# First three attention units' scores between the last three query projections, first keys by halves, values queued later

## The chip, the cores and the metric

The kernel runs on one core of one Trainium2 chip. The metric is the device time of one execution in microseconds (us). Below, TensorE is the matrix engine (PE in the profile, PEld its weight loads), VectorE is DVE, ScalarE is ACT, GpSimd is POOL, and SyncE (SP) issues most DMAs. GpSimd issues DMAs too, from a software queue of its own. PSUM is the accumulator memory of eight banks into which TensorE writes.

## What is computed

One layer of a diffusion backbone over 1024 latent tokens and 256 context tokens of width 1024: a modulated norm, one input projection whose columns feed two head groups (retention in both directions, and differential attention), an output projection, and a gated MLP with a short convolution. The change concerns differential attention and what stands just before it:

```
def diff_attention(q, k, v, lam):
    # q (B,H,2,Lq,d), k (B,H,2,Lk,d), v (B,H,Lk,dv), scale = d ** -0.5
    def attend(qb):
        s = jnp.einsum('bhmqd,bhmkd->bhmqk', qb, k).astype(jnp.float32) * scale
        p = jax.nn.softmax(s, axis=-1)
        a = p[:, :, 0] - lam * p[:, :, 1]
        return jnp.einsum('bhqk,bhke->bhqe', a.astype(v.dtype), v)
```

There are 4 heads (H), each with two maps of width d = 64, values of width 128, 1024 queries and 1280 keys (256 of the context, 1024 latent). The queries are projections of the normalised tokens, turned by a rotary embedding.

## The kernel before

The program is one long stream. A scheduler puts the instructions of a stretch in an order of its own unless they are tied to each other (`order_only`, `in_order`), and adds every wait that the data or a reused buffer needs.

**The stretch ahead of attention.** `transposed` computes the queries of differential attention. For one head h and one half hf of the tokens (512 columns) it sums eight k steps into one PSUM tile `pl`; a k step is three matmuls (`passes`, L131 to L133), since every operand is split into a high and a low part (`hT` tokens, `whi` and `wlo` weights). This document writes (h, hf) for such a projection. The last three, `by_head[-TAIL:]` with TAIL = 3, are (2,1), (3,0) and (3,1). `rotated` then turns each of them: ScalarE copies two halves of 64 partitions of `pl` into `xb` (L429), VectorE forms `xa` from `pl` (L431), `xb` is multiplied (L432, on GpSimd for the last three), VectorE adds (L433), and `split_store` splits `xa` into `xhl` (ScalarE cast L416, subtraction L417) and stores it to `dq_d` in DRAM by a DMA of SyncE (L418).

While the projections run, a generator beside them (`beside`, one step per `tick`, one tick per k step) issues the work of the other head group. In the last stretch its pairs of retention chunks end with `turn`: TensorE transposes into `pyt` (L286), ScalarE casts into `yr` (L290), VectorE subtracts (L291), SyncE stores `yr` (L293). `yr` has one buffer, so a cast waits until the store of the pair before has read it.

**Attention.** It runs in 32 units, one for each head and each 128 queries; unit u has head u // 8 and query tile u % 8. The steps of a unit are named by letters in `OPS`: S1 and S0 are the scores of map 1 and map 0 on TensorE (L874, six matmuls into `pA`, 1280 columns in three banks, twice for the high and low part of the query), M1 and M0 VectorE's minimum over a row (L877, a reduction; the scores are negated), E1 and E0 ScalarE's exponential with the sum of a row (L881, output `p`), R the ratio (L885, L886), C the combination of both maps (L889), T1, T2, T0 transposes of the result in groups of 512, 256 and 512 columns (L894 into `pt`), K1, K2, K0 their copies by ScalarE (L900 into `aT`), V0 to V2 the products with the values (L906 into `pv`); the rest normalises, with a power on GpSimd (`ssa`, L921), and writes the unit's rows into `yT`. Each map has one `pA` of three PSUM banks (`pss`), so S1 of a unit waits for E1 of the unit before.

In the loop the order is written out: `TAU` gives each step a time in units of one period, `order` sorts the steps of a period, and `in_order(start)` ties the instructions of TensorE, VectorE, ScalarE and SyncE to it. GpSimd is not tied.

**Before the loop** the first two units' steps up to C are issued by a generator beside the last three projections: `early` lets 15 ticks pass, and at the next one issues S1, M1, S0, M0, E1, E0, R, C of unit 0 and of unit 1 at once. Where they then stand is the scheduler's choice.

**Loads.** `load(i)` reads from DRAM, by GpSimd's queue, what unit i needs anew: every fourth unit the queries of four units (`qhl`, L953), every eighth the keys (`ks`, L956) and the values (`va`, L959) of a head. For unit 0 the queries and keys come in two parts for each map (four DMAs of 256 KB and four of 320 KB), then the values (640 KB). They are issued behind `last_y[0]`, the last product of the retention group on GpSimd.

**Output weights.** `out_weights` loads the first half of the output projection by GpSimd's queue (`woraw`, L998, four buffers), and splits it (ScalarE cast L1004, GpSimd subtraction L1005). Its steps are taken one for each period from the twelfth on, behind step f; the DMAs hang on nothing but their buffers.

## Time and profile before

| what | us |
|---|---|
| median of 3 runs | 1386.81 |
| lowest and highest | 1386.27, 1386.91 |
| the profiled execution, its own time | 1387.61 |
| its span, first to last instruction | 1385.8 |
| TensorE busy | 1367.0 |
| VectorE busy | 998.0 |
| ScalarE busy | 734.5 |
| GpSimd busy | 302.5 |
| granted TensorE clock, mean | 0.999 |

The prediction shows lines of these views. A page line of busy times gives for each engine the busy time, its share of the span and the number of instructions. A line of waits gives the engine, its tile and line, behind the arrow what it waited for, and then the total, the number and the longest of such waits. A timeline line gives the start, the duration, the engine, the line, the operation, output and inputs, their sizes, how many were merged (x6), and in brackets the idle time before it and what ended that. A DMA line gives output and input, the queue (SPq, POOLq), the count, the size of one and the time from issue to landing. A line of windows gives the stretch, its length, the busy time of TensorE, of its weight loads, of VectorE, ScalarE and GpSimd with instruction counts, the granted clock, the DMA engines' busy share and the GB/s moved. All times of lines are counted from the span's start.

Attention begins near 454 us, its loop near 470 us, and it ends near 655 us.

### The profile page before, as it was taken

The numbers are of one execution on the slowest core, as the hardware profiler recorded it, in microseconds if no ns is written. First come the engines' busy times: TensorE is split into PE (matmuls) and PEld (weight loads), VectorE is DVE, ScalarE is ACT, GpSimd is POOL, SyncE is SP. The second block draws the span as 40 slices with busy tenths as digits, with TensorE's granted clock in tenths as the row PEclk, the third lists the DMA queues.
The fourth block names the chain that finished last, engine by engine and source line by source line (L and its number), as shares of the span: only waits on it lengthen the run. The fifth ranks groups of instructions, "written<-read, shape, count | busy, mean of one in ns | idle before, by whom it ended". The sixth has DMA issues, their size and how long they took to land. (4 is left out here: it accounts for less than half of the span.)

```text
span 1385.8 us, 19518 instructions
## 1 busy us (share of the span) xinstructions
PE 1367.0 (99%) x7066; PEld 1149.5 (83%) x7066; DVE 998.0 (72%) x1474; ACT 734.5 (53%) x1400; POOL 302.5 (22%) x323
## 2 busy tenths in 40 slices
PE   9999999999999999999999999999999999999997
PEld 6788888888988799998888788888888888888886
DVE  4655774424776898895458998887778777799857
ACT  4652322434665789987136654555445555454534
POOL 1310000002656423411200643222332220000001
PEclk9999999999999999999999999999999999999999
DMA  9546885454564778622410232332323325963523
GB/s 371 204 167 208 294 271 184 145 176 141 156 189 143 214 176 185 142 50 93 174 69 23 99 109 105 114 114 92 114 99 114 104 71 177 376 229 110 180 91 122
DMA packets 95625, 214.63 MB, mean 155 GB/s; under 512 B 9317, under 2 KB 29797, under 8 KB 95017
## 3 DMA queue, kind: packets, MB, share of 16 engines
q1 hardware_dynamic: 86792, 187.03, 39.4%
q0 software_dynamic: 8160, 24.91, 7.8%
q10 hardware_dynamic: 576, 1.44, 0.3%
q8 instruction: 56, 0.92, 0.3%
q14 instruction: 41, 0.33, 0.1%
HBM read 158.03 MB, written 55.31 MB: 154 GB/s over the span
## 5 line engine op out<-in xcount | busy, mean ns | idle before, releaser
L131 PE MATMUL pl<-hT,whi 128*128 128x512 f32 x256 | 105.8, 413 | 0.0
L131 PE MATMUL chain<-T,whi 128*128 128x512 f32 x264 | 103.0, 391 | 1.2 <-ACT ub L1305 0.9
L132 PE MATMUL chain<-T,whi 128*128 128x512 f32 x264 | 102.8, 389 | 0.0
L133 PE MATMUL chain<-T,wlo 128*128 128x512 f32 x264 | 102.4, 389 | 0.0
L133 PE MATMUL pl<-hT,wlo 128*128 128x512 f32 x256 | 100.3, 392 | 0.0
L132 PE MATMUL pl<-hT,whi 128*128 128x512 f32 x256 | 99.9, 390 | 0.0
L877 DVE TENSOR_REDUCE mt<-pA 128x1 f32<-128x1280 f32 x64 | 95.2, 1490 | 4.1 <-PE pA L874 2.4
L874 PE MATMUL pA<-ks,qhl 128*128 128x512 f32 (+1 forms) x384 | 89.7, 369 | 1.2 <-DVE xa L431 0.9
L131 PE MATMUL c<-whi,ghl 128*128 128x512 f32 x232 | 90.2, 389 | 0.0
L132 PE MATMUL c<-wlo,ghl 128*128 128x512 f32 x232 | 90.2, 389 | 0.0
L133 PE MATMUL c<-whi,ghl 128*128 128x512 f32 x232 | 90.2, 389 | 0.0
L881 ACT ACTIVATE p<-pA,mt 128x1280 f32<-128x1280 f32 x64 | 85.5, 1336 | 5.9 <-DVE mt L877 4.7
L1051 ACT CAST whi<-cmb 128x512 fp32r<-128x512 f32 x62 | 38.5, 622 | 80.5 <-PE chain L132 62.9
L874 PEld LDWEIGHTS pA<-ks,qhl 128*128 128x128 f32 x384 | 67.8, 189 | 13.8 <-DVE xa L431 1.3
L906 PE MATMUL pv<-va,aT 128*128 128x128 f32 x640 | 77.0, 275 | 0.1
L1211 POOL TENSOR_TENSOR cmb<-wrb 128x512 f32<-128x512 f32 x19 | 28.0, 1476 | 221.8 <-DMA wrb<-w_up 143.4
L1054 DVE TENSOR_TENSOR wlo<-cmb,whi 128x512 fp32r<-128x512 f32 x62 | 60.1, 970 | 20.3 <-ACT whi L1051 20.2
L906 PEld LDWEIGHTS pv<-va,aT 128*128 128x128 f32 x640 | 74.0, 192 | 0.7 <-DVE yT L935 0.3
L1051 ACT CAST whi<-wra 128x512 fp32r<-128x512 f32 x54 | 33.2, 623 | 71.8 <-PE third L132 42.3
L131 PE MATMUL third<-yT,whi 128*128 128x512 f32 x168 | 65.4, 389 | 0.0
L132 PE MATMUL third<-yT,whi 128*128 128x512 f32 x168 | 65.4, 389 | 0.0
L133 PE MATMUL third<-yT,wlo 128*128 128x512 f32 x168 | 65.4, 389 | 0.0
(328 smaller groups left out, 3855.2 us busy)
## 6 DMA issues: line engine op xcount, KB each, us to landing
wm<-w_mod SPq DMA_DIRECT2D x32, 512.0 KB, 5.1
raw<-w_in SPq DMA_DIRECT2D x27, 512.0 KB, 4.9
wra<-w_up SPq DMA_DIRECT2D x24, 512.0 KB, 3.2
wrb<-w_up SPq DMA_DIRECT2D x22, 512.0 KB, 3.5
W<-w_down SPq DMA_DIRECT2D x44, 256.0 KB, 6.1
ad<-s SPq DMA_DIRECT2D x20, 512.0 KB, 3.4
wra<-ad SPq DMA_DIRECT2D x20, 512.0 KB, 3.3
kvs<-kvg SPq DMA_DIRECT2D x36, 256.0 KB, 3.1
```

Source lines behind the costliest of these rows:

```text
L131: mm(ps, lh, rh, start=first, stop=False, skip_group_check=more)
L132: mm(ps, lh, rl, start=False, stop=False, skip_group_check=more)
L133: return mm(ps, ll, rh, start=False, stop=last, skip_group_check=more)
L874: mm(self.pa[m][:, c0:c1], self.q[:, m, i, qs], self.k[:, m, c0:c1], start=(i == 0), stop=(i == 1))
L877: nc.vector.tensor_reduce(out=self.mt[:, m : m + 1], in_=self.pa[m][:, :LK], axis=AX.X, op=ALU.min)
L881: nc.scalar.activation(self.p[m], self.pa[m][:, :LK], AF.Exp, scale=-1.0, bias=self.mt[:, m : m + 1], accum_out=self.s[:, m : m + 1])
L906: mm(self.pv, self.aT[:, c, :], self.v[:, c, :], start=(c == 0), stop=(c == NKT - 1))
L1051: cast = nc.scalar.copy(hi, src)
L1054: nc.vector.tensor_tensor(out=lo, in0=src, in1=r32(hi), op=ALU.subtract)
L1211: nc.gpsimd.tensor_tensor(out=s1, in0=b1, in1=b2, op=ALU.add)
```

## The change

- `early` now makes three units and issues their first steps at set ticks (`AHEAD`): the key is the tick, the text the steps, with the unit's number ahead of the letter. Only TensorE's order of the stretch is tied (`in_order(begin, (PE,))`). Two more ties are added: C of unit 1 behind the last rotation (`newest_read`), and R behind M0 of unit 0.
- In the loop some steps of units 0, 2 and 3 move (`MOVED`): S0 of unit 2 takes the place of its S1, which went ahead, K1 and T2 of unit 0 go behind E1 of unit 2, and T0 and K0 of unit 0 behind S1 of unit 3.
- The two last turned pairs take their `yr` from the free buffers of `sc` and `qq`, two tiles that the retention group no longer needs.
- For unit 0 the queries come as the columns of units 0 and 1 for one map, then that map's keys, then the same for the other map, and the columns of units 2 and 3 last; these DMAs are tied to this order.
- `load_values(0)` issues the values of head 0 behind the first product that GpSimd does for a rotation, where they stood behind the keys.
- The pools `wo`, `at` and `psa` wait for the single tile whose place they take (`reuse_waits="tile"`), where they waited for all of the pool before.
- Each load of output weights is issued behind the power of unit n - 6.

```diff
...
 EARLY = ("S1", "M1", "S0", "M0", "E1", "E0", "R", "C")
+AHEAD = {13: "S1 M1", 15: "S0 M0 E1 E0", 17: "1S1 1M1 R C", 19: "1S0 1M0 1E1 1E0 1R 1C", 22: "2S1"}
...
+MOVED = {("S1", 2): [("S0", 2)], ("S0", 2): [], ("K1", 0): [], ("T2", 0): [], ("E1", 2): [("E1", 2), ("K1", 0), ("T2", 0)], ("T0", 0): [], ("K0", 0): [], ("S1", 3): [("S1", 3), ("T0", 0), ("K0", 0)]}
 FORCE = (mybir.EngineType.PE, mybir.EngineType.DVE, mybir.EngineType.Activation, mybir.EngineType.SP)
...
 
-    def in_order(start):
+    def in_order(start, engines=FORCE):
         last = {}
         for ins in nc.cur_bb.bb.instructions[start:]:
-            if ins.engine not in FORCE:
+            if ins.engine not in engines:
                 continue
...
                         order_only(ins.ins, behind.ins)
-                yr = rt.tile([P, 2, 2, P], F32R, name="yr", bufs=1)
+                left = H * NT // 2 - 1 - (self.h * NT // 2 + self.g)
+                yr = rt.tile([P, 2, 2, P], F32R, name="yr", bufs=1) if left > 1 else rt.tile([P, 2, 2, P], F32R, name="yr", tag=("qq", "sc")[left])
                 nc.scalar.copy(yr[:, 0], pt)
...
 
-        states_at, last_y, turned_q, newest = {}, [], {}, []
+        states_at, last_y, turned_q, newest, first_turned, newest_read, made = {}, [], {}, [], [], [], {}
 
...
             cs, sn = rtab[hf][:, 0, :], rtab[hf][:, 1, :]
-            nc.vector.scalar_tensor_tensor(out=xa, in0=pt, scalar=scale, in1=cs, op0=ALU.mult, op1=ALU.mult)
-            eng.tensor_tensor(out=xb, in0=xb, in1=sn, op=ALU.mult)
+            newest_read[:] = [nc.vector.scalar_tensor_tensor(out=xa, in0=pt, scalar=scale, in1=cs, op0=ALU.mult, op1=ALU.mult)]
+            turned_by = eng.tensor_tensor(out=xb, in0=xb, in1=sn, op=ALU.mult)
+            if eng is nc.gpsimd:
+                first_turned.append(turned_by)
             nc.vector.tensor_tensor(out=xa, in0=xa, in1=xb, op=ALU.add)
...
             h, qt = divmod(i, NT)
-            eng, ms = nc.gpsimd, ((1, 2), (0, 1)) if i == 0 else ((0, 2),)
+            eng = nc.gpsimd
             if qt % 4 == 0:
...
                 cur["k"] = alk.tile([P, 2, LK], F32R, name="ks")
-            for m0, m1 in ms:
+
+            def q_part(a, m0, m1, c0, c1):
+                return eng.dma_start(out=cur["q"][a * 64 : (a + 1) * 64, m0:m1, :, c0:c1], in_=dq_d[h][:, m0:m1, :, qt * P + c0 : qt * P + c1])
+
+            def k_part(a, m0, m1):
+                return eng.dma_start(out=cur["k"][a * 64 : (a + 1) * 64, m0:m1], in_=dk_d[h].rearrange("p m a l -> p a m l")[:, a, m0:m1])
+
+            if i == 0:
+                parts = []
+                for m in (1, 0):
+                    parts += [q_part(a, m, m + 1, 0, 2 * P) for a in range(2)]
+                    parts += [k_part(a, m, m + 1) for a in range(2)]
+                parts += [q_part(a, 0, 2, 2 * P, 4 * P) for a in range(2)]
+                for before, part in zip(parts, parts[1:]):
+                    order_only(part.ins, before.ins)
+                return dict(cur)
+            if qt % 4 == 0:
                 for a in range(2):
-                    if qt % 4 == 0:
-                        eng.dma_start(out=cur["q"][a * 64 : (a + 1) * 64, m0:m1], in_=dq_d[h][:, m0:m1, :, qt * P : (qt + 4) * P])
+                    q_part(a, 0, 2, 0, 4 * P)
+            if qt == 0:
                 for a in range(2):
-                    if qt == 0:
-                        eng.dma_start(out=cur["k"][a * 64 : (a + 1) * 64, m0:m1], in_=dk_d[h].rearrange("p m a l -> p a m l")[:, a, m0:m1])
-            if qt == 0:
-                cur["v"] = alv.tile([P, NKT, P], F32, name="va")
-                last_va[:] = [eng.dma_start(out=cur["v"], in_=dv_d[:, h * P : (h + 1) * P].rearrange("(c p) e -> p c e", p=P))]
+                    k_part(a, 0, 2)
+                load_values(h)
             return dict(cur)
+
+        def load_values(h):
+            cur["v"] = alv.tile([P, NKT, P], F32, name="va")
+            last_va[:] = [nc.gpsimd.dma_start(out=cur["v"], in_=dv_d[:, h * P : (h + 1) * P].rearrange("(c p) e -> p c e", p=P))]
 
...
         def early():
-            for _ in range(15):
-                yield
-            for u in range(2):
+            for u in range(3):
                 units[u] = Unit(u)
                 vars(units[u]).update(fore[u])
-                for op in EARLY:
-                    units[u].run(op)
+            for n in range(max(AHEAD) + 1):
+                for op in AHEAD.get(n, "").split():
+                    u = int(op[0]) if op[0].isdigit() else 0
+                    at = len(nc.cur_bb.bb.instructions)
+                    units[u].run(op[1:] if u else op)
+                    made[op] = nc.cur_bb.bb.instructions[at]
+                yield
 
         beside(early(), 1.0)
+        begin = len(nc.cur_bb.bb.instructions)
         transposed(wg, dq_d, rtab, 32, -DIFF_SCALE, 0, by_head[-TAIL:], eng=nc.gpsimd)
         beside(iter(()), 0.0)
+        in_order(begin, (mybir.EngineType.PE,))
+        order_only(made["1C"], newest_read[0].ins)
+        order_only(made["R"], made["M0"])
+        with tc.issue_after(first_turned[0].ins):
+            load_values(0)
+        for had in fore + [vars(units[u]) for u in range(3)]:
+            had["v"] = cur["v"]
         psl.close()
...
     ctx_wo = ctx.enter_context(ExitStack())
-    wo = ctx_wo.enter_context(tc.tile_pool(name="wo", bufs=1))
+    wo = ctx_wo.enter_context(tc.tile_pool(name="wo", bufs=1, reuse_waits="tile"))
 
...
     with ExitStack() as p2:
-        at = p2.enter_context(tc.tile_pool(name="at", bufs=2))
-        psa = p2.enter_context(tc.tile_pool(name="psa", bufs=1, space=PSUM))
+        at = p2.enter_context(tc.tile_pool(name="at", bufs=2, reuse_waits="tile"))
+        psa = p2.enter_context(tc.tile_pool(name="psa", bufs=1, space=PSUM, reuse_waits="tile"))
 
...
         for n in range(n_units + 8):
-            if 1 < n < n_units:
+            if 2 < n < n_units:
                 units[n] = Unit(n)
...
                 u = n - int(t)
-                if 0 <= u < n_units and (u > 1 or op not in EARLY):
+                if 0 <= u < n_units and (u > 1 or op not in EARLY) and (op, u) not in MOVED:
                     units[u].run(op)
+                for o, v in MOVED.get((op, u), ()):
+                    units[v].run(o)
                 if op == "f" and n >= 12:
-                    next(wo_gen, None)
+                    with tc.issue_after(units[min(n - 6, n_units - 1)].pool_ins.ins):
+                        next(wo_gen, None)
             if n + 3 < n_units:
...
                 with tc.issue_after(after.ins):
```

**TensorE, around the end of (3,0).** `hT_167` and `hT_169` are the high and low tokens of half 0, so rows with them belong to (3,0); `hT_168` and `hT_170` are half 1, (3,1). `pA` rows are one map's scores. Before:

```order
L131 MATMUL pl<-hT_167,whi 128x512
L132 MATMUL pl<-hT_169,whi 128x512
L133 MATMUL pl<-hT_167,wlo 128x512
L874 MATMUL pA<-ks,qhl 128x512 x4
L874 MATMUL pA<-ks,qhl 128x256 x2
L131 MATMUL pl<-hT_168,whi 128x512
L132 MATMUL pl<-hT_170,whi 128x512
L133 MATMUL pl<-hT_168,wlo 128x512
```

And now:

```order
L879 MATMUL pA<-ks,qhl 128x512 x4
L879 MATMUL pA<-ks,qhl 128x256 x2
L133 MATMUL pl<-hT_167,whi 128x512
L134 MATMUL pl<-hT_169,whi 128x512
L135 MATMUL pl<-hT_167,wlo 128x512
L133 MATMUL pl<-hT_167,whi 128x512
L134 MATMUL pl<-hT_169,whi 128x512
L135 MATMUL pl<-hT_167,wlo 128x512
L879 MATMUL pA<-ks,qhl 128x512 x4
L879 MATMUL pA<-ks,qhl 128x256 x2
L133 MATMUL pl<-hT_168,whi 128x512
```

S1 of unit 0 stood behind the last k step of (3,0) and now stands two k steps earlier; S0 stood two k steps into (3,1) and now stands behind (3,0). In (3,1) S1 of unit 1 now follows two k steps, its S0 four, S1 of unit 2 seven, and S0 of unit 2 all eight.

**ScalarE, from the halves of (2,1) on.** `pl_4262` is (2,1); (3,0) is `pl_4298` before and `pl_4304` now. `p1` and `p0` are the exponentials of map 1 and map 0. Before:

```order
L429 ACTIVATE xb_4288<-pl_4262 64x512 x2
L429 ACTIVATE xb_4376<-pl_4298 64x512 x2
L881 ACTIVATE p1_4341,sa_4324<-pA_4325,mt_4323 128x1280
L416 CAST xhl_4294<-xa_4287 128x512
L881 ACTIVATE p0_4343,sa_4324<-pA_4333,mt_4323 128x1280
L416 CAST xhl_4382<-xa_4375 128x512
L881 ACTIVATE p1_4367,sa_4350<-pA_4351,mt_4349 128x1280
L429 ACTIVATE xb_4412<-pl_4386 64x512 x2
L881 ACTIVATE p0_4369,sa_4350<-pA_4359,mt_4349 128x1280
```

And now:

```order
L432 ACTIVATE xb_4294<-pl_4262 64x512 x2
L432 ACTIVATE xb_4350<-pl_4304 64x512
L886 ACTIVATE p1_4345,sa_4267<-pA_4323,mt_4266 128x1280
L432 ACTIVATE xb_4350<-pl_4304 64x512
L886 ACTIVATE p0_4347,sa_4267<-pA_4337,mt_4266 128x1280
L419 CAST xhl_4300<-xa_4293 128x512
L419 CAST xhl_4356<-xa_4349 128x512
L886 ACTIVATE p1_4393,sa_4269<-pA_4367,mt_4268 128x1280
L886 ACTIVATE p0_4395,sa_4269<-pA_4385,mt_4268 128x1280
L432 ACTIVATE xb_4421<-pl_4360 64x512 x2
```

The first exponential now stands between the two halves of (3,0), and the halves of (3,1), the last row here, stand behind both exponentials of unit 1, where they stood ahead of the second.

**VectorE, from the rotation of (2,1) on.** Before:

```order
L431 SCALAR_TENSOR_TENSOR xa_4287<-pl_4262,rtab1_3755 128x512
L431 SCALAR_TENSOR_TENSOR xa_4375<-pl_4298,rtab0_3754 128x512
L877 TENSOR_REDUCE mt_4323<-pA_4325 128x1
L433 TENSOR_TENSOR xa_4287<-xa_4287,xb_4288 128x512
L877 TENSOR_REDUCE mt_4323<-pA_4333 128x1
L885 RECIPROCAL r_4345<-sa_4324 128x1
L433 TENSOR_TENSOR xa_4375<-xa_4375,xb_4376 128x512
L877 TENSOR_REDUCE mt_4349<-pA_4351 128x1
L886 SCALAR_TENSOR_TENSOR r_4345<-r_4345,sa_4324,nlam_144 128x1
L889 SCALAR_TENSOR_TENSOR p0_4343<-p1_4341,r_4345,p0_4343 128x1280
L877 TENSOR_REDUCE mt_4349<-pA_4359 128x1
```

And now:

```order
L434 SCALAR_TENSOR_TENSOR xa_4293<-pl_4262,rtab1_3755 128x512
L882 TENSOR_REDUCE mt_4266<-pA_4323 128x1
L434 SCALAR_TENSOR_TENSOR xa_4349<-pl_4304,rtab0_3754 128x512
L882 TENSOR_REDUCE mt_4266<-pA_4337 128x1
L438 TENSOR_TENSOR xa_4293<-xa_4293,xb_4294 128x512
L438 TENSOR_TENSOR xa_4349<-xa_4349,xb_4350 128x512
L882 TENSOR_REDUCE mt_4268<-pA_4367 128x1
L890 RECIPROCAL r_4375<-sa_4267 128x1
L891 SCALAR_TENSOR_TENSOR r_4375<-r_4375,sa_4267,nlam_144 128x1
L894 SCALAR_TENSOR_TENSOR p0_4347<-p1_4345,r_4375,p0_4347 128x1280
L882 TENSOR_REDUCE mt_4268<-pA_4385 128x1
```

The first reduction now stands ahead of the rotation of (3,0), the second behind it. Further on the rotation of (3,1) stands ahead of C of unit 1 in both, and behind the first reduction of unit 2 only now. On GpSimd the three `woraw` loads that stood ahead of unit 0's power (`ssa`) are gone from there.

## The prediction

> **What bounds the kernel now.** I read the page's busy times first, then TensorE's waits, then the timelines of TensorE, VectorE, ScalarE and the DMA issues around the place of the change.
>
> ```profile
> PE 1367.0 (99%) x7066; PEld 1149.5 (83%) x7066; DVE 998.0 (72%) x1474; ACT 734.5 (53%) x1400; POOL 302.5 (22%) x323
> ```
>
> TensorE is busy for 1367.0 of 1385.8 us. The change adds and removes no matmul, so it can only gain TensorE's idle time, 18.8 us in the whole program. TensorE's waits say how much of that lies near the change (engine, line, what it waited for: us in total, times, longest):
>
> ```profile
> PE pt L894 <- DVE xa L431: 1.0, 1, 1.0
> PE pA L874 <- DVE xa L431: 0.9, 1, 0.9
> PE pA L874 <- DMA ks<-dk: 0.2, 1, 0.2
> PE pA L874 <- ACT p L881: 0.2, 1, 0.2
> ```
>
> That is 2.3 us (1.0 + 0.9 + 0.2 + 0.2). The timeline shows where:
>
> ```profile
> 452.26 0.39 PE L131 MATMUL pl<-hT,whi 128*128 128x512 f32 x1
> 453.40 0.39 PE L133 MATMUL pl<-hT,wlo 128*128 128x512 f32 x1
> 454.66 1.40 PE L874 MATMUL pA<-ks,qhl 128*128 128x512 f32 x6 [0.87 <-DVE xa L431]
> 457.63 1.39 PE L874 MATMUL pA<-ks,qhl 128*128 128x512 f32 x6 [0.19 <-DMA ks<-dk]
> 465.33 1.31 PE L874 MATMUL pA<-ks,qhl 128*128 128x512 f32 x6
> 467.66 0.88 PE L894 MATMUL pt<-ident,p 128*128 128x128 f32 x6 [1.03 <-DVE xa L431]
> 470.51 1.43 PE L874 MATMUL pA<-ks,qhl 128*128 128x512 f32 x6 [0.16 <-ACT p L881]
> 472.21 2.40 PE L906 MATMUL pv<-va,aT 128*128 128x128 f32 x20
> 478.15 2.40 PE L906 MATMUL pv<-va,aT 128*128 128x128 f32 x20
> 484.48 2.40 PE L906 MATMUL pv<-va,aT 128*128 128x128 f32 x20
> 490.23 2.40 PE L906 MATMUL pv<-va,aT 128*128 128x128 f32 x20
> ```
>
> 452.26 and 453.40 are the first and last of the six matmuls that end projection (3,0): five steps in 1.14 us, 0.228 each, so a k step (three matmuls) is 0.68, and the scores of one map (2560 columns, five times 512) 1.14. An idle time also drains the array (a matmul lasts 0.39, the next starts after 0.228), so four of them are worth about 2.25 + 4 x 0.17 = 2.9. From value product to value product the first units take 5.94 and 6.33, the next 5.75: another 0.19 + 0.58 = 0.77 are lost in bubbles too short for the list of waits. **At most 2.9 + 0.8 = 3.7 us** can come back here.
>
> Which engine ends those waits? The same stage on VectorE:
>
> ```profile
> 455.11 0.69 DVE L431 SCALAR_TENSOR_TENSOR xa<-pl,rtab 128x512 f32<-128x512 f32 x1 [0.55 <-ACT xb L429]
> 456.09 1.49 DVE L877 TENSOR_REDUCE mt<-pA 128x1 f32<-128x1280 f32 x1 [0.28 <-PE pA L874]
> 464.00 1.55 DVE L889 SCALAR_TENSOR_TENSOR p<-p,r,p 128x1280 f32<-128x1280 f32 x1
> 465.46 1.49 DVE L877 TENSOR_REDUCE mt<-pA 128x1 f32<-128x1280 f32 x1
> 466.93 0.68 DVE L431 SCALAR_TENSOR_TENSOR xa<-pl,rtab 128x512 f32<-128x512 f32 x1
> 471.11 2.88 DVE L877 TENSOR_REDUCE mt<-pA 128x1 f32<-128x1280 f32 x2
> 474.43 1.55 DVE L889 SCALAR_TENSOR_TENSOR p<-p,r,p 128x1280 f32<-128x1280 f32 x1
> ```
>
> From 464.00 on VectorE runs without an idle note: this stage is a chain of VectorE and ScalarE, and TensorE waits for it. Successive operations overlap by some 0.09 (two reductions in 2.88), so a reduction costs the next one 1.40, a combination 1.46 (464.00 to 465.46), a 512-wide operation 0.60.
>
> **The change part by part.** *Buffers of the last turned pairs.* On ScalarE the last cast of yr waited 2.92 us for a store, and the halves of (2,1), whose products ended near 448.2 (452.26 less six k steps), came only at 452.64:
>
> ```profile
> 446.81 0.37 ACT L290 CAST yr<-pyt 128x256 fp32r<-128x256 f32 x1 [2.92 <-DMA yrd<-yr]
> 452.64 2.44 ACT L429 ACTIVATE xb<-pl 64x512 f32<-64x512 f32 x4
> 457.62 1.33 ACT L881 ACTIVATE p<-pA,mt 128x1280 f32<-128x1280 f32 x1 [2.54 <-DVE mt L877]
> 465.59 1.20 ACT L429 ACTIVATE xb<-pl 64x512 f32<-64x512 f32 x2 [1.00 <-PE pl L133]
> 470.36 0.61 ACT L416 CAST xhl<-xa 128x512 fp32r<-128x512 f32 x1
> ```
>
> With two free buffers that wait goes, (2,1) is turned by about 450.4, and nothing of it holds TensorE at 454.66 any more. What is late next is the first scores' load.
>
> *First keys by halves.* DMA issues (size, us to landing), and their times on GpSimd:
>
> ```profile
> qhl<-dq POOLq DMA_DIRECT2D x1, 256.0 KB, 4.3
> qhl<-dq POOLq DMA_DIRECT2D x1, 256.0 KB, 8.2
> ks<-dk POOLq DMA_DIRECT2D x1, 320.0 KB, 9.9
> ks<-dk POOLq DMA_DIRECT2D x1, 320.0 KB, 11.9
> va<-dvd POOLq DMA_DIRECT2D x1, 640.0 KB, 13.9
> 441.53 2.58 POOL L953 DMA_DIRECT2D qhl<-dq  x4
> 444.07 2.11 POOL L956 DMA_DIRECT2D ks<-dk  x4
> 475.97 1.70 POOL L998 DMA_DIRECT2D woraw<-w_out  x3 [3.63 <-DMA dq<-xhl]
> ```
>
> The first query part landed at 445.8 (441.5 + 4.3), the fourth DMA at 451.7 (443.5 + 8.2), the sixth, the last that map 1 needs, at 454.5 (444.6 + 9.9), the eighth at 457.5 (445.6 + 11.9, what TensorE waited for at 457.63). Now map 1 needs four DMAs with 896 KB where it needed 1664 KB. By bytes they land at 445.8 + 640/1408 x 8.7 = 449.8, by count at 451.7. Both lie before 452.26, where the scores now stand two k steps earlier. Map 0 needs all eight, 1792 KB: 455.3 by bytes, 457.5 by count, against 454.76. I take the former, nearest because the keys are unchanged and only query rows shrink; a delay up to 456.9 costs nothing, as the next step shows.
>
> *Scores spread in fixed order.* Map 1 of unit 0 starts at 452.26. Its scores last 1.31, the reduction runs to 455.06. (3,0) ends at 454.9 (452.26 + 1.14 + 2 x 0.68, plus the last matmul's drain). ScalarE then does, as the order shows, one half of (3,0) (0.60, to 455.6), the exponential (1.33, to 456.95) and only then the other half (to 457.55). VectorE's rotation of (3,0) waits for both halves, as it did at 455.11, and stands ahead of the second reduction. That starts at 457.6 + 0.6 = 458.2 and ends at 459.7, its exponential at 461.05, and unit 1's second scores, which reuse those banks, start at 461.2. TensorE is there at 454.76 + 1.14 + 1.37 + 1.14 + 1.37 = 459.8: **1.4 us idle**. From 458.2 VectorE runs on: reduction and two additions to 460.8, reduction 462.2, ratio 0.2, combination 463.85, reduction to 465.35; exponential to 466.7; unit 2's map 0 at 466.85, where TensorE is at 466.2: **0.65**. The halves of (3,1) follow on ScalarE to 467.9, its rotation to 468.65: unit 0's second group of transposes waits **0.1**. The exponential of unit 2 ends at 469.25, unit 3's scores wait **0.5**. The last cast of xhl, behind the addition that ends at 470.7, pushes unit 0's third copy to 471.9 (0.61 and about 0.57), the first value product **0.45** to 471.95. Before it was at 472.21, with the same products behind it: **0.26 us gained**. The old waits go, and 3.1 us of new ones come, because VectorE's work stays.
>
> On VectorE two reductions follow from 470.6, then ratio and combination of unit 2 at 473.8, where 474.43 stood: 0.6 earlier. So of the 0.77 us of bubbles in the next two units I take 0.35 as recovered (none if ScalarE sets them, 0.77 if VectorE does).
>
> The Trainium skill ("PSUM — Partial Sum Buffer", PSUM bank collisions raise a hardware error) says that ScalarE and VectorE may not touch one bank and quadrant at once, and that the scheduler orders such pairs; the trace agrees (0.55 us of waiting at 455.11). By it the split halves hold the rotation; without it the sum would be that of the first rival.
>
> *Values later.* Issued near 458.9, behind (3,0)'s turn on GpSimd. Landing by the old row at the worst 458.9 + 13.9 = 472.8, 0.85 after need; by the first query row's latency plus 640 KB at 320 KB per 1.4 us 458.9 + 4.3 + 2.8 = 466. The queue ahead is nearly empty then, so I take zero. *Output weights later, waits by tile.* 1.70 us of GpSimd issues leave 475.97, ahead of unit 0's power; no TensorE wait in the list names GpSimd, so it is inside the bubbles above. If the weights came late, their casts stand in order on ScalarE, but they have over two units (11.5 us) from issue. *Forced TensorE order* adds no instruction.
>
> The sum: 0.26 + 0.35 = 0.6 us. The profiled execution, 1387.61 us for a span of 1385.8, becomes 1387.0; it lies 0.8 above the median, which becomes 1386.81 - 0.6 = **1386.2 us**.
>
> **The rivals.** *The stalls really go.* If VectorE's second reduction need not wait for the split halves, it runs when its scores are done (456.1), the chain starts 2.1 us earlier, and time falls by 2.7 to 1384.1. For it: the list of waits has just these entries. Against it: the order on both engines and the row at 455.11. Chance 0.15.
>
> *Stores take the first keys' share (slower).* The last yr store and (2,0)'s store, no longer held back, now run among the loads.
>
> ```profile
> yrd<-yr SPq DMA_DIRECT2D x1, 256.0 KB, 4.8
> yrd<-yr SPq DMA_DIRECT2D x1, 256.0 KB, 12.5
> 450.00:452.00 2.00, 2.00 (x10) 1.69 (x9) 1.16 (x2) 1.49 (x2) 0.00 (x0) 1.00 1.12 280
> ```
>
> Such a store took 4.8 us when the loads began and 12.5 among them, so each side slows the other. 768 KB more (256 + 512) at 280 GB/s are 2.8 us; on top of the bound by count the keys land at 454.5. From 452.26 on every microsecond counts in full, since (3,0)'s own last steps stand behind those scores: 2.2 idle, 1386.2 + 2.2 = 1388.4. Against it: by bytes there are 2.4 us of slack. Chance 0.17, with a tail beyond 0.2% if the casts of yr and xhl then wait for stores too. The Trainium skill ("DMA: Bandwidth & Descriptors", Queues, rings and completion order) has each DMA engine take turns between its queues packet by packet; the 12.5 us agree.
>
> *Nothing moves.* VectorE's chain is what it was, the bubbles stay: 1386.8. Chance 0.13; the rest, 0.55, is the forecast.
>
> **How the numbers follow.** A change under 0.2%, 2.8 us, is about what a measurement of this kernel cannot tell from none. Faster than 1384.0 needs the first rival and a little of the bubbles: 0.12. Slower than 1389.6 needs the slow rival's tail: 0.10. Within: 0.78. The range takes in the first rival's price and most of the slow one's: 1384.0 to 1388.2. The forecast alone lies between 1385.5 and 1387.0.
>
> **What would show it.** TensorE's list should lose both waits on L431 and gain waits of scores on the exponentials, near 1.4 and 0.65. ScalarE should show no wait on yrd<-yr for the last cast. VectorE should idle some 2.5 us before (3,0)'s rotation, 455.1 to 457.6, and not again until 467. The first score should start near 452.3 with no DMA named; a DMA there makes the slow rival right. The first value product should start near 472.0; at 470 the first rival is right. A different time after unit 3, or waits on GpSimd or on wohi, would make the prediction wrong.

## The result, and the profile after

| kernel | median us | lowest to highest | runs |
|---|---|---|---|
| before | 1386.72 | 1385.63 to 1387.58 | 21 |
| changed | 1388.86 | 1387.64 to 1390.08 | 21 |

The ratio is 1.0017, with a 95% interval of 1.0011 to 1.0023: the change makes the kernel **2.1 us slower**. The profiled execution of the changed kernel took 1388.56 us for a span of 1386.7. Line numbers move by 2 to 5 in the rows below (and by up to 3 more in the experiments): the scores L874 are L879 now, the reduction L877 is L882, the exponential L881 is L886, r L886 is L891, the combination L889 is L894, the copy of `aT` L900 is L905, the value products L906 are L911, and in the rotation L429, L431, L432 and L433 are L432, L434, L435 and L438.

TensorE's waits between 430 and 490 us in the changed kernel (engine, line, what it waited for: total, times, longest):

```profile
PE pA L879 <- ACT p L886: 3.6, 3, 2.0
PE pv L911 <- ACT aT L905: 0.8, 1, 0.8
```

Three of the four entries of the kernel before are gone: VectorE's `xa` (1.0 and 0.9) and the keys' DMA (0.2), 2.1 us together. The entry on the exponential grew from 0.2 to 3.6 us, and a new one of 0.8 us names a copy of `aT`. TensorE's timeline shows where:

```profile
441.04 0.38 PE L288 MATMUL pyt<-ident,y 128*128 128x128 f32 x2
451.49 1.30 PE L879 MATMUL pA<-ks,qhl 128*128 128x512 f32 x6
460.60 1.42 PE L879 MATMUL pA<-ks,qhl 128*128 128x512 f32 x6 [1.36 <-ACT p L886]
467.94 1.43 PE L879 MATMUL pA<-ks,qhl 128*128 128x512 f32 x6 [2.03 <-ACT p L886]
470.61 1.43 PE L879 MATMUL pA<-ks,qhl 128*128 128x512 f32 x6 [0.21 <-ACT p L886]
473.66 2.50 PE L911 MATMUL pv<-va,aT 128*128 128x128 f32 x20 [0.75 <-ACT aT L905]
479.43 2.40 PE L911 MATMUL pv<-va,aT 128*128 128x128 f32 x20
485.31 2.40 PE L911 MATMUL pv<-va,aT 128*128 128x128 f32 x20
```

The first row is the last transposition of the retention group, which stands ahead of everything that the change moves on TensorE. In the kernel before it starts at 441.82, here at 441.04:

```profile
441.82 0.38 PE L286 MATMUL pyt<-ident,y 128*128 128x128 f32 x2
```

That 0.78 us comes from earlier in the program and moves from one kernel to the next (440.64 to 442.13 over the kernels below), so stretches are counted from that row here, and called **the stage**. The third value product starts at 485.31 in the changed kernel (before: 484.48). So the stage up to it takes 485.31 - 441.04 = 44.27 us, where it took 484.48 - 441.82 = 42.66: 1.61 us longer. From there to the last value product, 165.62 and 165.65, nothing differs. The two profiled executions differ by 0.95 us, 1.61 less the 0.78 of the start and some 0.1 over; the medians differ by 2.14. The 0.5 us between 1.61 and 2.14 is within what two medians of such runs leave open.

The wait of 2.03 us at 467.94 (unit 2's S0, for unit 1's E0) is the largest. Its chain on VectorE and ScalarE, from the same execution:

```profile
456.96 0.69 DVE L434 SCALAR_TENSOR_TENSOR xa<-pl,rtab 128x512 f32<-128x512 f32 x1 [2.64 <-ACT xb L432]
461.83 0.62 DVE L891 SCALAR_TENSOR_TENSOR r<-r,sa,nlam 128x1 f32<-128x1 f32 x1
462.49 2.55 DVE L894 SCALAR_TENSOR_TENSOR p<-p,r,p 128x1280 f32<-128x1280 f32 x1
464.96 1.48 DVE L882 TENSOR_REDUCE mt<-pA 128x1 f32<-128x1280 f32 x1
469.81 2.06 DVE L894 SCALAR_TENSOR_TENSOR p<-p,r,p 128x1280 f32<-128x1280 f32 x1
471.80 0.68 DVE L438 TENSOR_TENSOR xa<-xa,xb 128x512 f32<-128x512 f32 x1
466.47 1.33 ACT L886 ACTIVATE p<-pA,mt 128x1280 f32<-128x1280 f32 x1 [3.31 <-DVE mt L882]
```

The first combination takes 2.55 us and the second 2.06, where both took 1.55 before; r takes 0.62 instead of the usual 0.22. Beside them GpSimd works:

```profile
461.13 2.55 POOL L420 TENSOR_TENSOR xhl<-xa,xhl 128x512 fp32r<-128x512 f32 x2 [1.23 <-ACT xhl L419]
469.25 1.27 POOL L435 TENSOR_TENSOR xb<-xb,rtab 128x512 f32<-128x512 f32 x1 [4.99 <-ACT xb L432]
470.49 2.04 POOL L922 TENSOR_TENSOR e<-sa 128x1 f32<-128x1 f32 x2
```

Its two subtractions for the low parts of (2,1) and (3,0) run from 461.13 to 463.68. The first ends near 462.4, as r does (462.45). The combination starts at 462.49, and its 1.55 us counted from the end of the second subtraction would end at 465.23; it ended at 465.04. So it made hardly any progress while GpSimd worked. At 470.49 it is the other way round: two products of 128 numbers, 0.40 us in the kernel before, take 2.04 while VectorE combines until 471.87 and adds until 472.48. In the kernel before the subtractions ran at 459.62 and 462.65, beside an addition (0.93 us) and r (0.97 us):

```profile
459.62 1.30 POOL L417 TENSOR_TENSOR xhl<-xa,xhl 128x512 fp32r<-128x512 f32 x1 [2.53 <-ACT xhl L416]
460.54 0.93 DVE L433 TENSOR_TENSOR xa<-xa,xb 128x512 f32<-128x512 f32 x1
462.65 1.30 POOL L417 TENSOR_TENSOR xhl<-xa,xhl 128x512 fp32r<-128x512 f32 x1 [1.15 <-ACT xhl L416]
462.99 0.97 DVE L886 SCALAR_TENSOR_TENSOR r<-r,sa,nlam 128x1 f32<-128x1 f32 x1
468.28 0.40 POOL L917 TENSOR_TENSOR e<-sa 128x1 f32<-128x1 f32 x2
```

### The profile page after: what moved, and what is told of

Its sections match the earlier page's. It is cut to its first block, busy times and chain, and to the rows that moved or that the text cites. A ratio compares the mean times of both kernels' runs of the same rounds, so it can differ in the third digit from the quotient of the medians.

```text
span 1386.7 us, 19524 instructions
## 1 busy us (share of the span) xinstructions
PE 1366.0 (99%) x7066; PEld 1149.3 (83%) x7066; DVE 999.6 (72%) x1474; ACT 733.9 (53%) x1400; POOL 304.1 (22%) x325
## 3 DMA queue, kind: packets, MB, share of 16 engines
q10 hardware_dynamic: 576, 1.44, 0.3%
## 5 line engine op out<-in xcount | busy, mean ns | idle before, releaser
L882 DVE TENSOR_REDUCE mt<-pA 128x1 f32<-128x1280 f32 x64 | 95.1, 1489 | 6.1 <-PE pA L879 5.9
L879 PE MATMUL pA<-ks,qhl 128*128 128x512 f32 (+1 forms) x384 | 89.6, 369 | 3.6 <-ACT p L886 3.6
L886 ACT ACTIVATE p<-pA,mt 128x1280 f32<-128x1280 f32 x64 | 85.5, 1335 | 6.7 <-DVE mt L882 4.2
L879 PEld LDWEIGHTS pA<-ks,qhl 128*128 128x128 f32 x384 | 67.9, 189 | 16.1 <-ACT p L886 4.7
L911 PE MATMUL pv<-va,aT 128*128 128x128 f32 x640 | 77.0, 276 | 0.8 <-ACT aT L905 0.8
L911 PEld LDWEIGHTS pv<-va,aT 128*128 128x128 f32 x640 | 74.0, 192 | 1.7 <-ACT aT L905 1.3
```

The lines of the kernel that those rows point to most:

```text
L879: mm(self.pa[m][:, c0:c1], self.q[:, m, i, qs], self.k[:, m, c0:c1], start=(i == 0), stop=(i == 1))
L882: nc.vector.tensor_reduce(out=self.mt[:, m : m + 1], in_=self.pa[m][:, :LK], axis=AX.X, op=ALU.min)
L886: nc.scalar.activation(self.p[m], self.pa[m][:, :LK], AF.Exp, scale=-1.0, bias=self.mt[:, m : m + 1], accum_out=self.s[:, m : m + 1])
L911: mm(self.pv, self.aT[:, c, :], self.v[:, c, :], start=(c == 0), stop=(c == NKT - 1))
```

## The experiments

**Three theories.** Theory 1: VectorE's operations with two inputs in SBUF, the on-chip memory, and GpSimd's tensor operations hold each other up, and the change put GpSimd's subtractions beside the first combination, on the chain that TensorE waits for. Theory 2, the rival: the order on ScalarE costs it, E1 of unit 0 between the two halves of (3,0), so that VectorE idles 2.64 us before 456.96; the prediction had counted this cost, at 1.4 us of TensorE's time. Theory 3: one of the other edits costs it. In the diffs a kernel's own edit is shown against the changed kernel, or against the kernel before where its name begins with b. Lines that only keep an instruction in a list are left out: `halves[1]` is ScalarE's second copy for (3,0), `lows[-3:-1]` are GpSimd's subtractions for (2,1) and (3,0). The kernel before, run beside each set of experiments, took 1386.75 to 1387.00 us there, so a few tenths of a microsecond between an experiment and the changed kernel say nothing.

### a_nosub and b_nosub: GpSimd's subtractions left out

```diff
-            eng.tensor_tensor(out=hl[:, 1, :n], in0=src, in1=r32(hl[:, 0, :n]), op=ALU.subtract)
-            nc.sync.dma_start(out=dst.rearrange("p m a l -> (p m) a l"), in_=r32(hl[:, :, :n]))
+            if eng is not nc.gpsimd:
...
+            else:
+                nc.sync.dma_start(out=dst.rearrange("p m a l -> (p m) a l"), in_=r32(hl[:, 0:1, :n]).to_broadcast([P, 2, n]))
```

> The changed kernel with GpSimd's three subtractions (the low parts of the last three projections' query blocks) left out and the high part stored in their place. Nothing else moves on any engine. Theory 1 (VectorE's operations with two SBUF inputs and GpSimd's tensor operations hold each other up): the ratio r of unit 0 goes from 0.62 to 0.22 us and the first combine from 2.55 to 1.55, the second combine stays near 2.06 because the multiplication of xb still runs beside it; the wait of unit 2's S0 on the exps goes from 2.03 to about 0.65; the kernel loses about 1.4 us, to about 1387.4 where the changed kernel took 1388.9. Theory 2 (the order of E1 between the halves of (3,0) costs it): combine 2.55 as before or shorter, but the time stays within 0.4 us of 1388.9, since GpSimd is not on the chain. Theory 3 (other parts: yr buffers, tile waits, later values): stays within 0.4 us.

> The kernel before with the same three GpSimd subtractions left out, high part stored in their place; the control for a_nosub. Theory 1: here they fall beside short VectorE operations (an addition of 0.93 instead of 0.69 us, a ratio of 0.97 instead of 0.22) in the stage where PE waits 0.9 and 1.0 us for the additions of xa, so it gains 0.3 to 1.0 us, to about 1386.1; less than the 1.4 in the changed kernel. Theory 2 and 3: no change beyond 0.4 us here as there. If it gains as much as a_nosub (1.4 or more), the subtractions do not tell the two kernels apart.

All three subtractions are left out, and the high part is stored in place of the low part as well. a_nosub took 1387.53 us, 1.33 less than the changed kernel, and its stage 42.87, 1.40 less. VectorE and TensorE in a_nosub:

```profile
461.99 0.22 DVE L894 SCALAR_TENSOR_TENSOR r<-r,sa,nlam 128x1 f32<-128x1 f32 x1
462.24 1.55 DVE L897 SCALAR_TENSOR_TENSOR p<-p,r,p 128x1280 f32<-128x1280 f32 x1
466.70 1.43 PE L882 MATMUL pA<-ks,qhl 128*128 128x512 f32 x6 [0.63 <-ACT p L889]
468.51 2.06 DVE L897 SCALAR_TENSOR_TENSOR p<-p,r,p 128x1280 f32<-128x1280 f32 x1
```

r and the first combination are back at 0.22 and 1.55, the wait fell from 2.03 to 0.63, and the second combination, beside which the multiplication of xb still runs, stays at 2.06. All four as theory 1 has it. b_nosub took 1386.60 us beside 1386.79 for the kernel before (ratio 0.9996, 0.9987 to 1.0005): 0.2 us, under the 0.3 to 1.0 that was expected, and not told from nothing. Its stage, though, took 41.07 us, 1.59 less than the 42.66 of the kernel before. Of that, 1.02 stand already at the first score, ahead of the first subtraction that is left out:

```profile
453.37 1.39 PE L877 MATMUL pA<-ks,qhl 128*128 128x512 f32 x6
453.76 0.69 DVE L434 SCALAR_TENSOR_TENSOR xa<-pl,rtab 128x512 f32<-128x512 f32 x1 [2.03 <-ACT xb L432]
```

The score starts 11.82 us into the stage here and waits for nothing; in the kernel before, with the same loads, it starts at 12.84, behind a wait of 0.87. The second DMA of the keys took 9.0 us to land here and 9.9 there. So these loads land about a microsecond sooner or later, and the profiled execution of the kernel before, 0.9 us above its kernel's median, had a late one. The other 0.57 us of the 1.59 were not taken apart. By the medians the subtractions cost the changed kernel 1.3 us and the kernel before 0.2; what differs is beside what they run, and the next experiment takes that alone.

### a_subC: the subtractions kept, but started when the combination has ended

```diff
+        seen = nc.gpsimd.tensor_tensor(out=al.tile([P, 1], F32, name="seen", bufs=1), in0=units[0].p[0][:, 0:1], in1=mhalf[:, 0:1], op=ALU.mult)
+        for low in lows[-3:-1]:
+            order_only(low.ins, seen.ins)
```

> The changed kernel, whole, with the subtractions of (2,1) and (3,0) on GpSimd queued behind a one-column read of the first combine's output, so that they start when it has ended (about 463.6 us instead of 461.1) and run beside VectorE's least of unit 1, which reads PSUM. Theory 1: first combine 1.55 and ratio 0.22 us; a gain of about 1.4 us, to 1387.4; the reductions keep 1.48 us. If the reductions over PSUM stretch beside GpSimd too, the gain is under 0.5. Theory 2 and 3: within 0.4 us of 1388.9.

```profile
461.82 1.55 DVE L894 SCALAR_TENSOR_TENSOR p<-p,r,p 128x1280 f32<-128x1280 f32 x1
463.29 1.48 DVE L882 TENSOR_REDUCE mt<-pA 128x1 f32<-128x1280 f32 x1
463.61 2.52 POOL L420 TENSOR_TENSOR xhl<-xa,xhl 128x512 fp32r<-128x512 f32 x2
```

The combination took 1.55 us, the reduction beside the subtractions 1.48, and the wait of unit 2's S0 was 0.60. The stage took 42.92 us, 1.35 less. Nothing is left out here, so the place of GpSimd's work alone is worth this. The time fell to 1388.43 only, by 0.4, where 1387.4 was expected: from the third value product to the last it took 166.13 us instead of 165.62. There a unit takes 5.78 instead of 5.75, although no instruction of that stretch was edited. c_both below makes the same read into a tile that exists already and has 165.60, so it is the new tile, not the read. Why a new tile costs this is not shown.

### a_tieE1: E1 behind both halves of (3,0)

```diff
+        order_only(made["E1"], halves[1].ins)
```

> The changed kernel with ScalarE's exp E1 of unit 0 queued behind the second half of (3,0)'s copy instead of between the two halves. Theory 2: the rotation of (3,0) on VectorE starts at about 455.0 instead of 456.96, and everything behind it on VectorE by up to 2 us earlier; E1 and E0 end about 0.7 later or the same; the wait of 1S0 (1.36) stays because it waits for E0, and that of S0 of unit 2 falls from 2.03 to under 1; the kernel gains 1 to 2 us. Theory 1: the rotation starts earlier, but the chain is ScalarE's E1, E0 and then VectorE's combine of 2.55 beside GpSimd's subtractions; the time stays within 0.5 us of 1388.9, or the collision moves to another operation.

It took 1387.23 us, 1.6 less, and its stage 42.82, 1.45 less. ScalarE, VectorE and TensorE in a_tieE1:

```profile
454.35 1.20 ACT L432 ACTIVATE xb<-pl 64x512 f32<-64x512 f32 x2 [5.41 <-PE pl L135]
455.57 0.69 DVE L436 SCALAR_TENSOR_TENSOR xa<-pl,rtab 128x512 f32<-128x512 f32 x1 [1.18 <-ACT xb L432]
461.10 2.55 DVE L896 SCALAR_TENSOR_TENSOR p<-p,r,p 128x1280 f32<-128x1280 f32 x1
457.04 1.43 PE L881 MATMUL pA<-ks,qhl 128*128 128x512 f32 x6 [0.27 <-ACT p L888]
466.55 1.43 PE L881 MATMUL pA<-ks,qhl 128*128 128x512 f32 x6 [1.64 <-ACT p L888]
```

The rotation starts 1.44 us earlier in the stage (14.48 instead of 15.92). The first map of unit 1 now waits 0.27 for the later E1, and 1S0's wait of 1.36 is gone, against the expectation, which had it stay. The wait of unit 2's S0 fell less than expected, from 2.03 to 1.64 instead of under 1, and the combination still takes 2.55, as theory 1 has it. So each theory names a real cost, and the two lie on one chain.

### a_Mfirst: the reduction ahead of the combination

```diff
+        order_only(made["C"], made["1M0"])
```

> The changed kernel, whole, with the first combine C of unit 0 queued behind the least 1M0 of unit 1 on VectorE, where the change has it ahead; nothing else moves but the second unit's ratio, one place. If what unit 2's S0 waits for is 1M0 held up by the stretched combine in front of it, 1M0 starts at about 462.1 instead of 464.96, 1E0 at 463.6, S0 of unit 2 waits 0 instead of 2.03, the combine runs from 463.6 in 1.55 us as GpSimd's subtractions have ended, and the time falls by 1.5 to 2.0 us, to 1386.9 to 1387.4. If GpSimd stretches the reduction over PSUM as it does the combine, or if the combine is what PE's turns wait for, the wait moves to the turns and the time stays within 0.5 us of 1388.9.

It took 1387.18 us, 1.7 less, and its stage 42.38, 1.89 less. VectorE and TensorE's waits in a_Mfirst:

```profile
462.49 1.48 DVE L882 TENSOR_REDUCE mt<-pA 128x1 f32<-128x1280 f32 x1
463.89 1.54 DVE L894 SCALAR_TENSOR_TENSOR p<-p,r,p 128x1280 f32<-128x1280 f32 x1
```

```profile
PE pA L879 <- ACT p L886: 1.5, 2, 1.3
PE pv L911 <- ACT aT L905: 0.8, 1, 0.8
PE pt L899 <- DVE xa L434: 0.5, 1, 0.5
```

The reduction reads PSUM and keeps 1.48 us beside GpSimd's second subtraction; the combination, started behind it, takes 1.54. Unit 2's S0 waits no more, and 0.5 us come back where unit 0's transposes wait for the rotation of (3,1), the wait of 1.0 us in the kernel before. What TensorE waited for was the reduction behind the stretched combination, not the combination.

### a_whole, a_norest and a_yr1: the other edits, undone

In a_whole the first queries and keys come as before the change; six more ties, not shown, hold VectorE's and ScalarE's order to that of the changed kernel:

```diff
                 for m in (1, 0):
-                    parts += [q_part(a, m, m + 1, 0, 2 * P) for a in range(2)]
+                    parts += [q_part(a, m, m + 1, 0, 4 * P) for a in range(2)]
+                for m in (1, 0):
                     parts += [k_part(a, m, m + 1) for a in range(2)]
-                parts += [q_part(a, 0, 2, 2 * P, 4 * P) for a in range(2)]
```

a_norest takes back the buffers of yr, `reuse_waits="tile"` of `wo`, `at` and `psa`, and the place of the output weights' loads; a_yr1 the buffers of yr alone.

> The changed kernel with the first keys and queries loaded as before the change (four pieces of queries, then four of keys, each whole) and the order of VectorE and ScalarE held as in the changed kernel; PE's order is the same. The first score stands at 10.45 us behind the last turned block of the retention there, and at 12.84 us, with a wait of 0.87, in the kernel before. If that wait of 0.87 was for VectorE's rotation, as the prediction had it, the first score waits for nothing here and the time stays within 0.4 us of 1388.9. If it was for the first keys (the trace of b_nosub shows no wait at all at the same place with the rotation still ahead), the first score waits 0.5 to 2.0 us for a DMA here and the time is 0.5 to 2.0 us over 1388.9.

> The changed kernel with the other edits undone: one buffer of yr, the pools wo, at and psa with their old waits, the output weights' loads not queued behind GpSimd. Theories 1 and 2 (the loss lies in the first units' chain): within 0.5 us of 1388.9. Theory 3 (one of these parts costs it): 1 to 2 us less, 1387 to 1388.

> The changed kernel with one edit undone: the last two blocks of yr take one buffer again. All the other edits undone together cost 1.04 us (a_norest, 1389.90). If the wait of ScalarE's copy on the store of yr is what they gained, this alone takes 0.6 to 1.1 us more than 1388.9. The prediction took this wait at nothing: then it stays within 0.4 us, and the gain lies in the pools' waits and the output weights' loads, which the trace of a_norest shows as 0.5 us more between the second and the third unit's values.

| kernel | us | against the changed kernel | stage up to the third value product |
|---|---|---|---|
| a_whole | 1389.78 | +0.9 | 45.87 |
| a_norest | 1389.90 | +1.0 | 45.02 |
| a_yr1 | 1389.08 | +0.2 | 44.27 |

TensorE's waits in a_whole:

```profile
PE pA L880 <- ACT p L887: 3.3, 2, 2.0
PE pA L880 <- DMA ks<-dk: 1.1, 1, 1.1
PE pv L912 <- ACT aT L906: 0.2, 1, 0.2
```

Theory 3 falls for the edits that were undone: they gain. The edits of the first loads spare 1.1 us of waiting at the first score. Whether the halves of the keys do that alone is open, since a_whole also issues the values 8 us earlier in the stage, behind GpSimd's first multiplication instead of its second:

```profile
449.78 1.05 POOL L983 DMA_DIRECT2D va<-dvd  x1
458.24 1.04 POOL L982 DMA_DIRECT2D va<-dvd  x1
```

(The first row is a_whole, the second the changed kernel.) The pools' waits and the output weights' loads spare about 0.8 (1.0 less 0.2), of which 0.5 show between the second and the third value product of a_norest, and the buffers of yr next to nothing. The forced order of TensorE, the third unit made ahead and `MOVED` were not undone. a_yr1 and a_norest show one thing more: with yr's wait back, (2,1) is turned late again, at 451.68 and 452.54, and the first score, at 451.15 and 452.00, stands ahead of that and waits for nothing.

### c_both: both edits

```diff
+        order_only(made["E1"], halves[1].ins)
+        seen = nc.gpsimd.tensor_tensor(out=warm[:, 1:2], in0=units[0].p[0][:, 0:1], in1=mhalf[:, 0:1], op=ALU.mult)
+        for low in lows[-3:-1]:
+            order_only(low.ins, seen.ins)
```

> The changed kernel with both earlier edits: E1 behind the second half of (3,0), and GpSimd's subtractions of (2,1) and (3,0) behind the first combine, here read into a tile that exists already. If the two costs are separate steps of one chain (the order of ScalarE 1.4 us, the collision 1.4 us) and add, the wait of unit 2's S0 goes from 2.03 us to under 0.4 and the one of 1S0 from 1.36 to about 0.3, and the time is 2.0 to 2.6 us under the changed kernel: 1386.3 to 1386.9. If both edits remove the same wait, the time stays at that of the better one alone, 1387.2.

> c_both again, the same program: 1386.0 to 1386.4, beside a fresh set of runs of the kernel before; with the first set it tells whether the version with both edits is under the kernel before.

c_both took 1386.07 us and c_both2 1385.96, with 1386.75 and 1387.00 for the kernel before beside them: ratios 0.9997 (0.9988 to 1.0005) and 0.9993 (0.9984 to 1.0001). That is 2.8 and 2.9 us under the changed kernel, more than the 2.0 to 2.6 that was expected, and 0.7 and 1.0 under the kernel before, which neither interval alone tells from no change. The stage took 41.42 and 41.39 us, 1.2 less than in the profiled execution of the kernel before with its late keys, but 0.3 more than in b_nosub, which has the old order without the subtractions; so a gain on the kernel before is not shown. TensorE's waits in c_both:

```profile
PE pv L913 <- ACT aT L907: 0.8, 1, 0.8
PE pA L881 <- ACT p L888: 0.7, 3, 0.3
```

The 3.6 us of waits on exponentials are 0.7, and the gains add: 1.35 and 1.45 alone, 2.85 together.

### c_cast and c_cast2: the two places left

c_cast is c_both with ScalarE's cast of (3,1) behind the third copy of `aT`. c_cast2, whose lines are shown, also queues GpSimd's multiplication of (3,1) behind the second combination and VectorE's addition of it behind two reductions; c_cast has the line with `casts` alone.

```diff
+        seen = nc.gpsimd.tensor_tensor(out=warm[:, 2:3], in0=units[1].p[0][:, 0:1], in1=mhalf[:, 0:1], op=ALU.mult)
+        order_only(first_turned[2].ins, seen.ins)
...
+        order_only(casts[-1].ins, copies[2].ins)
+        order_only(adds[-1].ins, least[6].ins)
```

> c_both with ScalarE's cast of the last projection's high part queued behind the third copy of aT, where it stood ahead of it and waited 1.2 us for VectorE. If the wait of 0.76 us of the first values is that copy held up by the cast, the wait goes to under 0.2 and the time falls by 0.5 to 0.8 us under c_both, to 1385.3 to 1385.6. If the copy itself waits for the turned blocks or the combine, the wait stays and the time is within 0.3 of 1386.1.

> c_cast with GpSimd's multiplication of the last projection queued behind the second combine (by a one-column read of its output) and VectorE's addition of it behind the two leasts that follow. Theory 1 (one engine's operation holds the other's up until it has ended): the second combine takes 1.55 instead of 2.06 us and the e products beside it 0.2 each instead of a stretched 2.04 for both; the leasts keep 1.48. On the path: 0 to 0.6 us less than c_cast, 1384.9 to 1385.5. If the second combine keeps 2.06, its length has another cause than GpSimd.

They took 1386.26 and 1386.28 us: no gain on c_both, where 1385.3 to 1385.6 and 1384.9 to 1385.5 were expected. In c_cast the wait of the first values fell from 0.76 to 0.24 and that product started 29.31 us into the stage instead of 29.78, but the second one at 35.57 instead of 35.54 and the third at 41.43 instead of 41.42: what came free was given back within one unit. In c_cast2 VectorE and GpSimd show:

```profile
467.86 1.54 DVE L896 SCALAR_TENSOR_TENSOR p<-p,r,p 128x1280 f32<-128x1280 f32 x1
469.62 1.27 POOL L437 TENSOR_TENSOR xb<-xb,rtab 128x512 f32<-128x512 f32 x1
470.85 0.34 POOL L924 TENSOR_TENSOR e<-sa 128x1 f32<-128x1 f32 x2
473.30 1.55 DVE L896 SCALAR_TENSOR_TENSOR p<-p,r,p 128x1280 f32<-128x1280 f32 x1
473.55 2.44 POOL L420 TENSOR_TENSOR xhl<-xa,xhl 128x512 fp32r<-128x512 f32 x1 [2.36 <-ACT xhl L419]
```

The second combination is back at 1.54 and the two small products at 0.34, as theory 1 has it, and the time does not move. But the collision is not gone: it comes one unit later, where GpSimd's last subtraction meets the third combination and takes 2.44 us instead of 1.27. So these runs do not show whether the collision at the second combination cost anything; at the first one, a_nosub and a_subC show that it does.

## Why the prediction was wrong

**Right.** The old waits went, and new ones of scores on exponentials took their place: 1.36 us at 1S0, where 1.4 was forecast. VectorE idles 2.64 us before the rotation of (3,0), by the split halves that the order showed. ScalarE's last cast of yr waits for no store, and undoing this alone changes little (a_yr1). The first score waits for no DMA, which ends the slow rival; that the measured time lies close to that rival's 1388.4 is luck. The values, issued at 458.24, are named in no wait. The bubbles between the first three value products fell from 12.27 to 11.65 us, 0.62 gained where 0.35 was taken.

**The step that failed** is "combination 463.85": the working took every operation of VectorE at its undisturbed length (1.46 for a combination, from 464.00 to 465.46). The order of GpSimd's subtractions against VectorE's combination was not looked at. They fell on each other: r and the combination took 0.40 and 1.00 us more, the reduction behind them came as much later, and the wait of unit 2's S0 was 2.03 instead of 0.65. a_nosub takes that one cost away and finds 0.63 there. That corrects the sum by 1.4 us; the wait of the first values was 0.75 instead of 0.45, for the second combination was stretched too. With it the whole list of new waits is 4.35 us (1.36 + 2.03 + 0.21 + 0.75) instead of 3.1. The first value product was forecast 0.26 us earlier in the stage, and came 2.23 later (473.66 - 441.04 = 32.62, before 472.21 - 441.82 = 30.39). a_nosub, without the subtractions, has it 1.38 earlier than the changed kernel, at 31.24 (472.42 - 441.18). So the other 1.1 of these 2.5 us are not theirs. A part of that is the term "ratio 0.2", too small by 0.3: the reciprocal and r took 0.52 us in a_nosub (461.72 to 462.24), as those of unit 2 did in the kernel before (473.91 to 474.43). Another 0.3 is the longer wait of the first values. The rest lies in small delays, such as the transposes at 469.21 that took 1.18 us where 0.88 stood, and was not taken apart.

In medians the forecast was 1386.2, a_nosub took 1387.53 and the changed kernel 1388.86: the collision is half of the miss. Without it the kernel would still not have been faster than before (ratio 1.0005, 0.9996 to 1.0014). A second weakness of the sum can hold some of the other half: it counted the wait of 0.9 us at the first score as lost in the kernel before, and took the gain off the median, but b_nosub has no such wait with the same loads. How much of it the median execution has was not measured.

The rows that could have told were in the trace of before: r took 0.97 us at 462.99 and the addition 0.93 at 460.54, beside GpSimd's subtractions, and 0.21 and 0.68 elsewhere. The Trainium skill ("SBUF — State Buffer", Who interferes with whom) has the rule: a VectorE instruction with two inputs in SBUF contends with a GpSimd instruction that reads SBUF, and the second to issue is blocked until the first is done, while a reduction on this chip never contends. The trace agrees on each point, but for some 0.2 us in which the two overlapped: 2.55 for 1.55 us where GpSimd was first, 2.04 for 0.40 on GpSimd where VectorE was, and 1.48 for the reduction beside GpSimd in a_subC. As a rival in the prediction it would have given about 1 us for a combination and 0.4 for r, and so 1387.6 instead of 1386.2, inside the stated range and still 1.3 under the measured time.

**Right for the wrong cause.** The list of waits named VectorE's `xa` for the 0.9 us at the first score of the kernel before, and the prediction followed it: it had the freed yr buffers remove that wait. Two things ended together there: the rotation of (2,1), begun at 453.87, at 454.56, and the keys' second DMA at 454.5 by the prediction's own sum; the list names one. a_norest, a_yr1 and b_nosub have the late rotation behind their first score, and no wait there. In b_nosub the score started at 453.37, just after the keys landed (issued near 444.2, 9.0 us), and a_whole, with (2,1) turned early and whole loads, waits 1.1 us for the keys. So these runs put the wait down to the loads, and what removed it to the edits of the loads. The other wait on `xa`, 1.0 us at the transposes, was VectorE's: it comes back with 0.5 us in a_Mfirst.

**The rivals.** None was it. "The stalls really go" needed the reduction free of the split halves, and a_tieE1 shows that they did hold it; even with the collision gone as well, c_both and c_both2 stay 2.0 and 1.9 us over that rival's 1384.1. "Nothing moves" and the stores fall with the waits above. Loss by two engines holding each other up was not among them, so the range ended 0.7 us below the median.

## What to carry to other kernels

When an order is rewritten on the engines that wait, look up what the untied engine does at the new places: here GpSimd's work was the same, and cost 1.3 us beside a combination that TensorE's next product depended on, and 0.2 us, not told from nothing, beside short operations. Take the length of an operation from a row that has the same neighbours, and read a row that is longer than its kind as a sign of a resource shared with whatever runs beside it. A fixed order also fixes what stands behind a stretched operation: putting the reduction that the next engine waits for ahead of the combination gained no less than removing the collision (1.7 and 1.3 us). And a wait that is read from one execution can be that execution's own: the list of waits named one engine, where the runs put the wait down to a load that landed about a microsecond late.

## What the runs showed of the hardware that had not been expected

- GpSimd's tensor operations and VectorE's operations with two SBUF inputs hardly overlapped in these traces (by some 0.2 us where the first combination met the subtractions), however small the second one was: r, of 128 numbers, went from 0.22 to 0.62 us. In each such pair that was looked at here the one that started second took longer: VectorE's combination 2.55 us instead of 1.55, GpSimd's two products 2.04 instead of 0.40.
- One more tile of 4 bytes a partition (a_subC) made a unit of the unchanged loop 5.78 instead of 5.75 us long, 0.5 us over the loop; the cause stays open.
- With the same loads the second DMA of the first keys took 9.9 us to land in the kernel before and 9.0 in b_nosub, and the first score started 1.0 us later in the stage.
- 0.5 us gained at the first value product (c_cast) were gone at the second, with TensorE idle 0.2 us for a copy of `aT` in between; what sets that pace was not tried.
